# Third experts with a fully split down projection, routing without GpSimd's subtractions, and weights stored as whole 4 KB tiles

## The chip, the cores and the metric

One core of a Trainium2 chip runs the whole program. The metric is the device time of that core in microseconds (us), from the start to the end of one execution. The kernel of before ran three times: 2966.38, 2972.29 and 2977.92 us, median 2972.29.

Engines are named as the profile names them: PE (TensorE, matmuls), PEld (its weight loads), DVE (VectorE), ACT (ScalarE), POOL (GpSimd), SP (SyncE, which issues most DMAs).

## What is computed

The reference runs two different transformer blocks, each of two layers, over 256 tokens of 1024 features, all in float32. The change lies in the first block, mostly in its mixture of experts:

```python
h = rms_norm(x, norm_ffn[l]) * (1.0 + scale_f) + shift_f
grp_idx = top_k(softmax(h @ w_router_grp + b), 1)          # one of 4 groups
top_logit, top_idx = top_k(exp_logits of that group, 2)    # 2 of its 8 experts
for g in range(4):                                         # 32 experts in all
    a, u = h @ w_gate[g], h @ w_up[g]                      # 1024 -> 256
    y += (silu(a) * u * comb[:, g]) @ w_down[g]            # 256 -> 1024
x = x + gate_f * y
```

Ahead of it stands a mixer (`h @ w_in`, attention and gated linear attention, `@ w_out`). The second block has a mixer with its own `w_in_2` and a PEER layer with queries `x @ peer_wq_2` and two tables of 16384 rows.

## The kernel before

**Split products.** PE multiplies float32 in a fast form (F32R) if the operands are rounded. So a weight tile of 128 x 1024 that lands as `raw` is split: ACT copies it rounded to `wh` (L147), DVE or POOL writes `wl = raw - wh` (L150), and PE multiplies with both parts. A weight used without a split ("plain") goes to PE as float32 and costs PE more, but ACT and DVE nothing.

**The stream of weights.** `Stream` knows the order of all weight tiles from a dry run. `load` issues DMAs on SP as soon as a raw buffer is free (10 in the first block, 12 more lent to the experts). `pop` hands out the next tile and, before that, issues the splits of up to `ahead` (4) tiles beyond it, into six pairs of `wh`/`wl`. `prepare(n, engine)` does so at a chosen place and with a chosen engine for the subtraction. Each engine runs its instructions in the order in which they are written; the order of the program is the schedule.

**Planning the experts (`moe_plan`).** Rows are squared and summed on ACT (`square`), X is transposed on PE, four ACT and four DVE instructions (L967, L965) bring it out of PSUM, 32 products with the router weights give the logits (DVE scales them and adds the shift's part at L983). Meanwhile `parts` makes the normalised rows and splits them: two ACT instructions (L957, L958) and one POOL subtraction (L959) per half. Three `prepare` calls split five weight tiles, one subtraction on DVE and four on POOL. `route` (L875 to L898) is a chain of small DVE instructions; its result `m` (L988) is what PE waits for. Then tokens are placed in a sorted order by permutation products (`sorted_half`), and the first expert's gate and up products run between the two halves.

**The experts (`moe_experts`).** The 32 experts of a layer run in one loop, two to a pair `q` that shares 64 rows of sorted tokens. `pick(q + 1)` takes the next pair's rows: an ACT copy (L1120) and a POOL subtraction (L1121) give `hsel`. Six weight tiles belong to an expert: four for gate and up (each 4 x 256 columns in rows of 1 KB in DRAM), two for `w_down`. `expert_down` multiplies the first `w_down` tile split and the second one plain:

```python
parts = w(0)                       # wh, wl: four F32R products of 512 columns
whole = w(1)                       # raw: two float32 products
s.mm(y[n][:SL], h[1], whole[:, n * 512:n * 512 + 512], ...)
```

`hidden` (L1134) makes its other operand: ACT's silu (L1140), DVE's product with the up half (L1141), and the split of the first half of the hidden features alone (L1142, L1143). At e = 1 `weights_of_slots` issues eight DVE instructions (`first`, `gs`, L1178 and L1181) that need a chain of ten small POOL instructions (L1075 to L1084); at e = 2 PE multiplies them, after the gate and up products of half 0 of e = 2. `hsel` of pair 1 is first picked at e = 0, behind those ten POOL instructions on POOL's queue. `most > SL` guards a path (`overflow`) for experts with more than 64 tokens; with these inputs it does not run.

In the trace the planning and the experts take 203 to 532 us in layer 0 and some 691 to 1030 us in layer 1.

## Time and profile before

| | before |
|---|---|
| runs, median (lowest to highest) | 2972.29 us (2966.38 to 2977.92) |
| the profiled execution: its time | 2973.85 us |
| its span, first to last instruction | 2972.1 us |
| PE busy | 2822.3 us, 95% |
| DVE busy | 2235.5 us, 75% |
| ACT busy | 1594.1 us, 54% |
| POOL busy | 490.2 us, 16% |
| mean granted PE clock | 0.968 |
| moved by DMA | 618 MB, 208 GB/s |

Busy means that an instruction of the engine ran. A wait is idle time of an engine that an instruction on another engine ended (the releaser). Only PE's idle time and what stretches its instructions counts directly here; another engine's time counts where PE waits for it. A DMA share is the mean busy share of the core's 16 DMA engines; it can pass 1 where packets overlap.

### The profile page before, as it was taken

Reading aid. Unit: us, or ns where it says so; the run is one execution under the profiler, and the core shown is the slowest. Engines: PE = TensorE matmul, PEld = TensorE weight load, DVE = VectorE, ACT = ScalarE, POOL = GpSimd, SP = SyncE. Lnnn points to the kernel's source line nnn. Section 1 sums busy time; section 2 is a strip of 40 time slices with the busy share of each in tenths; the row PEclk is TensorE's granted clock in tenths of the full one; section 3 lists DMA queues with packets and bytes.
Section 4 is the critical chain, followed back from the end, with each engine's and each line's share of the span. In section 5 each row is a group of like instructions: output and inputs, shape, how many; then the busy total and the mean of one; then the engine's idle time right before and its main releaser. Section 6 shows DMA issues by size and latency. Waiting matters only on the chain. (4 is left out here: it accounts for less than half of the span.)

```text
span 2972.1 us, 48339 instructions
## 1 busy us (share of the span) xinstructions
PE 2822.3 (95%) x18290; PEld 2438.0 (82%) x18291; DVE 2235.5 (75%) x3730; ACT 1594.1 (54%) x2576; POOL 490.2 (16%) x350
## 2 busy tenths in 40 slices
PE   7888999897999989999999999998999999999998
PEld 7766777776777677999999788878799999978886
DVE  7778988767888765898898655566589989865555
ACT  3446777555677546554544444454655554444444
POOL 1222322113322232311000100003331100010000
PEclk9989999998999989999999999998999999999999
DMA  9677998656999442555455555554255554555554
GB/s 355 223 256 259 373 361 301 207 171 228 320 366 360 160 130 72 180 188 175 158 164 169 203 192 191 191 172 138 79 179 188 176 165 162 171 198 191 206 191 149
DMA packets 290588, 618.07 MB, mean 208 GB/s; under 512 B 25168, under 2 KB 159120, under 8 KB 290080
## 3 DMA queue, kind: packets, MB, share of 16 engines
q1 hardware_dynamic: 288816, 608.92, 60.7%
q0 software_dynamic: 1520, 5.87, 0.6%
q8 instruction: 149, 2.44, 0.3%
q14 instruction: 103, 0.84, 0.1%
HBM read 611.30 MB, written 3.15 MB: 207 GB/s over the span
## 5 line engine op out<-in xcount | busy, mean ns | idle before, releaser
L150 DVE TENSOR_TENSOR wl<-raw,wh 128x1024 fp32r<-128x1024 f32 x919 | 1157.5, 1282 | 406.7 <-ACT wh L147 403.0
L147 ACT ACTIVATE wh<-raw 128x1024 fp32r<-128x1024 f32 (+1 forms) x983 | 1006.3, 1050 | 411.9 <-PE pair L245 364.3
L243 PE MATMUL bank<-xth,wh 128*128 128x256 f32 x2048 | 577.0, 282 | 0.0
L245 PE MATMUL bank<-xth,wl 128*128 128x256 f32 x2048 | 571.3, 279 | 0.4 <-DVE wl L150 0.4
L244 PE MATMUL bank<-xtl,wh 128*128 128x256 f32 x2048 | 571.1, 279 | 0.0
L245 PE MATMUL pair<-wh,al 128*128 128x512 f32 x1024 | 401.0, 392 | 10.8 <-DVE al L239 10.8
L243 PE MATMUL pair<-wh,ah 128*128 128x512 f32 x1024 | 403.2, 394 | 1.6 <-ACT ah L238 1.6
L244 PE MATMUL pair<-wl,ah 128*128 128x512 f32 x1024 | 400.9, 392 | 0.0
L245 PEld LDWEIGHTS bank<-xth,wl 128*128 128x128 f32 x2048 | 387.7, 189 | 1.0 <-DVE wl L150 0.8
L243 PEld LDWEIGHTS bank<-xth,wh 128*128 128x128 f32 x2048 | 386.9, 189 | 0.0
L244 PEld LDWEIGHTS bank<-xtl,wh 128*128 128x128 f32 x2048 | 385.5, 188 | 0.0
L248 PE MATMUL bank<-wh,hsel 128*128 128x256 f32 x1024 | 263.7, 296 | 12.8 <-POOL hsel L1121 12.0
L248 PE MATMUL bank<-wl,hsel 128*128 128x256 f32 x1024 | 250.9, 283 | 1.0 <-POOL wl L150 1.0
L248 PEld LDWEIGHTS bank<-wh,hsel 128*128 128x128 f32 x1024 | 194.8, 190 | 67.6 <-issue 25.3
L245 PEld LDWEIGHTS pair<-wh,al 128*128 128x128 f32 x1024 | 192.6, 188 | 57.6 <-DVE al L239 14.1
L243 PEld LDWEIGHTS pair<-wh,ah 128*128 128x128 f32 x1024 | 192.7, 188 | 43.3 <-ACT ah L238 2.3
L244 PEld LDWEIGHTS pair<-wl,ah 128*128 128x128 f32 x1024 | 192.7, 188 | 41.1
L150 POOL TENSOR_TENSOR wl<-raw,wh 128x1024 fp32r<-128x1024 f32 (+2 forms) x67 | 161.0, 2405 | 379.1 <-ACT wh L147 373.0
L248 PEld LDWEIGHTS bank<-wl,hsel 128*128 128x128 f32 x1024 | 195.4, 191 | 2.7 <-POOL wl L150 1.2
L243 PE MATMUL pair<-xth,wh 128*128 128x256 f32 x512 | 150.5, 294 | 0.0
L245 PE MATMUL pair<-xth,wl 128*128 128x256 f32 x512 | 147.4, 288 | 0.7 <-POOL wl L150 0.7
L244 PE MATMUL pair<-xtl,wh 128*128 128x256 f32 x512 | 148.0, 289 | 0.0
(517 smaller groups left out, 4675.5 us busy)
## 6 DMA issues: line engine op xcount, KB each, us to landing
raw<-in_peer_ut SPq DMA_DIRECT2D x256, 512.0 KB, 3.6
raw<-in_peer_v SPq DMA_DIRECT2D x256, 512.0 KB, 3.3
raw<-in_w_gate SPq DMA_DIRECT2D x128, 512.0 KB, 7.5
raw<-in_w_up SPq DMA_DIRECT2D x128, 512.0 KB, 6.9
raw<-in_w_down SPq DMA_DIRECT2D x128, 512.0 KB, 6.2
raw<-in_w_ada SPq DMA_DIRECT2D x96, 512.0 KB, 5.2
raw<-in_w_in SPq DMA_DIRECT2D x80, 512.0 KB, 4.6
raw<-in_w_out SPq DMA_DIRECT2D x32, 512.0 KB, 3.6
```

What stands on the lines that cost most here:

```text
L147: nc.scalar.activation(b, a, AF.Copy)
L150: engine.tensor_tensor(c, a, b.bitcast(F32), op=ALU.subtract)
L243: return [mm(out, lhsT=lh, rhs=rh, start=start, stop=False, skip_group_check=True), mm(out, lhsT=lh, rhs=rl, start=False, stop=False, skip ...
L244: mm(out, lhsT=lh, rhs=rl, start=False, stop=False, skip_group_check=True),
L245: mm(out, lhsT=ll, rhs=rh, start=False, stop=stop, skip_group_check=True)]
L248: s.nc.tensor.matmul(out, lhsT=lhsT, rhs=rhs, start=start, stop=stop, skip_group_check=True)
```

## The change

- Every expert with `e % 3 == 2` (e = 2, 5, ... 29; ten of 32 in each layer) has its second `w_down` tile split as well, and both halves of its hidden features; the other 22 keep the plain product.
- In `moe_plan` the two subtractions of `parts` go to DVE, and both squares and the first half's `parts` go ahead of the transposes' evacuation, the second half's behind it. The `prepare` calls on POOL go away: one tile is split ahead of the route, one after the places of the tokens, two inside `sorted_half(1)`, all on DVE.
- `pick` of pair 1 moves from e = 0 in `moe_experts` to `moe_plan`, behind the first expert's products and ahead of the ten POOL instructions. `hsel1` gets a buffer that outlives the plan.
- `w_gate`, `w_up`, `w_in`, `w_in2` and `peer_wq_2` are laid out by the host so that each tile of 128 x 1024 is one contiguous block with a 4 KB row per partition. Before, a partition's 4 KB came as four pieces of 1 KB (gate, up) or two of 2 KB (the others). The tiles hold the same numbers.

```text
instructions per layer   before                  after
w_down second tile       32 plain                22 plain, 10 split
subtractions of parts    2 on POOL               2 on DVE
early splits             1 on DVE, 4 on POOL     4 on DVE
```

The diff, without the guarded path and the list of input names:

```diff
@@ -353,30 +353,33 @@
         return [(lambda t: t, s.A["w_ada"][l, k * P:(k + 1) * P, j * D:(j + 1) * D])], "plain"
     def w_in(s, name, l, c, n=512):
-        w = s.A[name]
+        w = s.A[name if n == 512 else name + "_rest"]
         def tile_of(i):
+            if n == 512:
+                return [(lambda t: t, w[l, c, i])], 1024
             return [(lambda t: t.rearrange("p (k n) -> p k n", k=2)[:, :, :n],
-                     w[l, i * 256:i * 256 + 256, c * 512:c * 512 + n].rearrange("(k p) n -> p k n", p=P))], \
-                1024 if n == 512 else -n
+                     w[l, i].rearrange("p (k n) -> p k n", k=2))], -n
         return tile_of
     def w_lr(s, l):
-        return [(lambda t: t[:, :128].rearrange("p (k n) -> p k n", k=8),
-                 s.A["w_in"][l, :, 3072:3088].rearrange("(k p) n -> p k n", p=P))], 128
+        return [(lambda t: t[:, :128], s.A["w_lr"][l])], 128
     def w_rows(s, name, l, k):
         return [(lambda t: t, s.A[name][l, k * P:(k + 1) * P, :])], 1024
     def w_expert(s, name, l, e, half):
-        w = s.A[name][l, e % 4, e // 4]
-        return [(lambda t: t.rearrange("p (k n) -> p k n", k=4),
-                 w[half * 512:half * 512 + 512, :].rearrange("(k p) n -> p k n", p=P))], 1024
+        return [(lambda t: t, s.A[name][l, e % 4, e // 4, half])], 1024
     def w_expert_down(s, l, e, k):
-        return [(lambda t: t, s.A["w_down"][l, e % 4, e // 4, k * P:(k + 1) * P, :])], "plain" if k else 1024
+        return [(lambda t: t, s.A["w_down"][l, e % 4, e // 4, k * P:(k + 1) * P, :])], \
+            "plain" if k and s.whole(e) else 1024
+
+    def whole(s, e):
+
+        return e % 3 != 2
     def ada_pe(s, l, j, n):
@@ -956,8 +959,14 @@
             h, lo = (q[:, tt].rearrange("p (k n) -> p k n", k=4) for q in (xh, xl))
             nc.scalar.activation(x, y, AF.Copy, scale=ss[:, tt:tt + 1])
             nc.scalar.activation(h, x, AF.Copy)
-            nc.gpsimd.tensor_tensor(lo, x, h.bitcast(F32), op=ALU.subtract)
+            yield
+            nc.vector.tensor_tensor(lo, x, h.bitcast(F32), op=ALU.subtract)
+            yield
         square(0)
+        square(1)
+        low = parts(0), parts(1)
+        next(low[0])
+        next(low[0])
         banks = s.transposes(s.X)
         for k in range(KT):
             z = banks[k // 2][:, k % 2]
@@ -965,12 +974,9 @@
                 nc.vector.tensor_scalar(ht[:, k], z, g[:, k:k + 1], None, op0=ALU.mult)
             else:
                 nc.scalar.activation(ht[:, k], z, AF.Copy, scale=g[:, k:k + 1])
-        square(1)
+        next(low[1])
+        next(low[1])
         s.st.prepare(1 + ADA_PE, nc.vector)
-        s.st.prepare(2 + ADA_PE, nc.gpsimd)
-        parts(0)
-        parts(1)
-        s.st.prepare(5 + ADA_PE, nc.gpsimd)
         b = s.bank().rearrange("p (t n) -> p t n", t=2)
         for k in range(KT):
             for tt in range(2):
@@ -1048,12 +1054,14 @@
         nc.vector.tensor_copy(oc, pb[:, 2:4])
         each = oc.rearrange("p a (q two) -> p a q two", two=2)
         nc.vector.tensor_copy(offi, each[:, 0, :, 0])
+        s.st.prepare(2, nc.vector)
         next(weights)
         s.table("silu_and_others")
         for _ in sorted_half(0):
             pass
         rest = sorted_half(1)
         next(rest)
+        s.st.prepare(4, nc.vector)
         gu = s.bank()
         s.gate_up(gu, hsel, 0, s.expert_weights(l, 0, 1))
         for _ in rest:
@@ -1062,6 +1070,7 @@
         for j, op in enumerate((ALU.is_lt, ALU.is_ge)):
             nc.vector.tensor_tensor(of_pair[:, j], s.slot[:, 0:1].to_broadcast([P, 16]), each[:, 1, :, 0], op=op)
         s.gate_up(gu, hsel, 1, s.expert_weights(l, 0))
+        following = s.pick(1, hs, offi, mkk)
         next(weights)
         rank, ok, key = mkk([P, 2, 2], "rank"), mkk([P, 2, 2], "ok"), mkk([P, 2, 2], "key")
...
@@ -1131,29 +1140,33 @@
                     s.mm(gu[:, name * 256:name * 256 + 256], hsel[:, k].rearrange("p a q -> p (a q)"), q[:, kk],
                          start=(k == 0 and name == 0 and i == 0), stop=(k == 7 and i == 1))
-    def hidden(s, gs, mk):
+    def hidden(s, whole, gs, mk):
         b = s.bank()[:, :4 * SL].rearrange("p (f q) -> p f q", f=4)
         for f in range(4):
             s.mm(b[:, f], gs[:, f * 128:f * 128 + 128], s.halves, start=(f == 0))
-        a, h = mk([P, 2, SL], "hid", bufs=2), mk([P, 2, SL], "hids", F32R, bufs=2)
+        a, h = mk([P, 2, SL], "hid", bufs=2), mk([P, 2, 2, SL], "hids", F32R, bufs=2)
+        n = 1 if whole else 2
         s.nc.scalar.activation(a, b[:, 0:2], AF.Silu)
         s.nc.vector.tensor_tensor(a, a, b[:, 2:4], op=ALU.mult)
-        s.nc.vector.tensor_copy(h[:, 0], a[:, 0])
-        s.nc.vector.tensor_tensor(h[:, 1], a[:, 0], h[:, 0].bitcast(F32), op=ALU.subtract)
+        s.nc.vector.tensor_copy(h[:, :n, 0], a[:, :n])
+        s.nc.vector.tensor_tensor(h[:, :n, 1], a[:, :n], h[:, :n, 0].bitcast(F32), op=ALU.subtract)
         return h, a[:, 1]
-    def expert_down(s, h, w, y, j):
-
-
-        parts = w(0)
-        for n in range(2):
-            for i, q in enumerate(parts):
-                s.mm(y[n], h[0].rearrange("p a q -> p (a q)"), q[:, n * 512:n * 512 + 512],
-                     start=(j == 0 and i == 0), stop=False)
-        whole = w(1)
-        for n in range(2):
-            s.mm(y[n][:SL], h[1], whole[:, n * 512:n * 512 + 512], start=False, stop=(j == 1))
+    def expert_down(s, h, w, y, j, whole):
+
+
+        for k in range(2):
+            first, last = k == 0 and j == 0, k == 1 and j == 1
+            parts = w(k)
+            for n in range(2):
+                c = slice(n * 512, n * 512 + 512)
+                if k and whole:
+                    s.mm(y[n][:SL], h[1], parts[:, c], start=False, stop=last)
+                    continue
+                for i, q in enumerate(parts):
+                    s.mm(y[n], h[0][:, k].rearrange("p a q -> p (a q)"), q[:, c], start=first and i == 0,
+                         stop=last and i == 1)
     def rows_at(s, idx):
         return idx if s.dry else bass.IndirectOffsetOnAxis(ap=idx, axis=0)
@@ -1209,8 +1222,8 @@
         def down(e):
-            s.expert_down(h, lambda k: s.st.pop(*s.w_expert_down(l, e, k), ahead=None if e < 30 else 63 - 2 * e - k),
-                          yb, e % 2)
+            s.expert_down(h, lambda k: s.st.pop(*s.w_expert_down(l, e, k),
+                                                   ahead=None if e < 30 else 63 - 2 * e - k), yb, e % 2, s.whole(e))
         def weighed(q):
             y, by = [[mk([P, 512], f"y{x}{n}", F32R) for x in "hl"] for n in range(2)], ws[:, q:q + 1]
@@ -1239,8 +1252,10 @@
             if e:
                 gu = s.bank()
                 s.gate_up(gu, hsel, 0, w)
-            if e % 2 == 0 and q < 15:
-                following = s.pick(q + 1, p["hs"], p["offi"], mkk if q % 2 else mk)
+            if e == 0:
+                following = p["following"]
+            elif e % 2 == 0 and q < 15:
+                following = s.pick(q + 1, p["hs"], p["offi"], mkk)
             if e % 2 == 0 and q >= 2:
                 add_all(q - 2)
             if e == 2:
@@ -1266,14 +1281,14 @@
             if e < 31:
                 gn = copied(e, gu)
             if e:
-                h = s.hidden(gs, mk)
+                h = s.hidden(s.whole(e - 1), gs, mk)
             gs = gn
             if e % 2:
                 hsel = following
                 if e < 28:
                     s.adas.tick()
                     s.reduces.tick()
-        last = s.hidden(gs, mk)
+        last = s.hidden(s.whole(31), gs, mk)
         hot = back(15)
         next(hot)
         add_all(14)
...
@@ -2238,9 +2252,23 @@
             nc.scalar.activation(d[:, first:], b[:, first:], AF.Copy, scale=1.0 / GATE)
+def tiles(w, k, n):
+
+
+    lead, (r, c) = w.shape[:-2], w.shape[-2:]
+    w = w.reshape(*lead, r // (k * P), k, P, c // n, n)
+    d = len(lead)
+    w = w.transpose(*range(d), d + 3, d, d + 2, d + 1, d + 4)
+    return np.ascontiguousarray(w).reshape(*lead, c // n, r // (k * P), P, k * n)
+
+
 def lay1(I):
     o = {}
+    o["w_in"] = tiles(I["w_in"][:, :, :3072], 2, 512)
+    o["w_lr"] = tiles(I["w_in"][:, :, 3072:], 8, 16)[:, 0, 0]
+    for name in ("w_gate", "w_up"):
+        o[name] = tiles(I[name], 4, 256)[:, :, :, 0]
     o["c_col"] = np.ascontiguousarray(I["c"].reshape(8, P).T)
     cols = []
     for l in range(2):
@@ -2283,7 +2311,9 @@
     o["cols2"] = np.ascontiguousarray(np.stack(cols))
     o["cmp_pos"] = np.ascontiguousarray(np.stack(pos))
     o["cmp_w1"] = np.ascontiguousarray(np.stack(w1))
-    o["w_in2"] = np.ascontiguousarray(np.stack(w))
+    w = np.stack(w)
+    o["w_in2"], o["w_in2_rest"] = tiles(w[:, :, :2048], 2, 512), tiles(w[:, :, 2048:], 2, 280)[:, 0]
+    o["peer_wq_2"] = tiles(I["peer_wq_2"], 2, 512)
     o["b_row2"] = np.ascontiguousarray(np.stack(rows))
     wo = I["w_out_2"]
     o["w_out2"] = np.ascontiguousarray(wo)
...
```

## Rows read from the trace of the kernel before

**Rows 1.** Busy by stretch (start:end length): PE PEld DVE ACT POOL, clock, DMA, GB/s.

```profile
15.00:20.00 5.00, 4.80 (x23) 4.71 (x24) 3.84 (x3) 0.00 (x0) 0.00 (x0) 1.00 1.02 418
...
232.00:238.00 6.00, 6.00 (x51) 5.76 (x50) 2.21 (x9) 5.08 (x10) 0.00 (x0) 1.00 0.51 169
280.00:300.00 20.00, 19.97 (x117) 14.69 (x116) 19.57 (x23) 13.14 (x18) 6.68 (x3) 1.00 1.07 373
300.00:500.00 200.00, 199.71 (x1187) 151.44 (x1186) 180.16 (x220) 148.45 (x193) 55.51 (x24) 1.00 1.05 364
```

**Rows 2.** PE's waits over the run: total us, times, longest.

```profile
PE bank L248 <- DVE m L988: 21.3, 2, 10.8
PE bank L248 <- POOL hsel L1121: 12.0, 2, 6.3
```

**Rows 3.** Timeline of DVE, routing in layer 0: start us, length us, instruction.

```profile
212.06 0.43 DVE L983 SCALAR_TENSOR_TENSOR lg<-bank,ss,lgc 128x40 f32<-128x40 f32 x2 [0.17 <-PE bank L248]
...
213.01 1.13 DVE L883 CAST gi<-i 128x2 f32<-128x2 uint32 x1
214.18 2.27 DVE L884 TENSOR_TENSOR goh<-iota,gi 128x8 f32<-128x8 f32 x1
216.49 2.33 DVE L887 TENSOR_TENSOR pick<-lg,goh 128x64 f32<-128x64 f32 x1
...
219.76 1.29 DVE L896 CAST ip<-i8b 128x4 f32<-128x4 uint32 x1
221.09 2.25 DVE L897 SCALAR_TENSOR_TENSOR ei<-ip,gi 128x4 f32<-128x4 f32 x1
223.38 2.39 DVE L898 TENSOR_TENSOR oh<-iota,ei 128x128 f32<-128x128 f32 x1
225.81 0.23 DVE L988 TENSOR_TENSOR m<-oh 128x64 bf16<-128x64 f32 x1
225.95 0.28 DVE L989 TENSOR_TENSOR at<-iota,ei 128x128 f32<-128x128 f32 x1
```

**Rows 4.** Timeline of POOL, the same stretch.

```profile
214.07 4.66 POOL L959 TENSOR_TENSOR xl<-hs,xh 128x1024 fp32r<-128x1024 f32 x2
218.69 6.93 POOL L150 TENSOR_TENSOR wl<-raw,wh 128x1024 fp32r<-128x1024 f32 x3
```

**Rows 5.** Timeline of ACT ahead of the logits.

```profile
206.53 1.57 ACT L967 ACTIVATE hs<-bank,affine 128x256 f32<-128x256 f32 x4 [1.12 <-PE bank L518]
207.97 1.07 ACT L951 ACTIVATE xl<-X 128x1024 fp32r<-128x1024 f32 x1
...
211.49 1.13 ACT L957 ACTIVATE hs<-X,ss 128x1024 f32<-128x1024 f32 x1
```

**Rows 6.** Timeline of PE, the products that give the logits.

```profile
207.57 4.45 PE L248 MATMUL bank<-wr,hs 128*128 128x40 f32 x32 [0.48 <-DVE hs L965]
```

**Rows 7.** Timeline of layer 0 around the first pick, POOL, DVE and PE.

```profile
254.05 2.14 POOL L1121 TENSOR_TENSOR hsel<-hs,hsel 128x512 fp32r<-128x512 f32 x2
...
256.59 0.28 DVE L1181 TENSOR_SCALAR gs<-ident,key 128x128 f32<-128x128 f32 x1
...
258.55 0.64 PE L248 MATMUL bank<-oh,first 128*128 128x32 f32 x5
```

**Rows 8.** Timeline of PE, one expert's down projection, and where the next-but-one's ends.

```profile
303.65 0.39 PE L248 MATMUL bank<-wh,hids 128*128 128x512 f32 x1
303.88 0.39 PE L248 MATMUL bank<-wl,hids 128*128 128x512 f32 x1
...
306.52 0.39 PE L248 MATMUL bank<-wh,hsel 128*128 128x256 f32 x1
...
324.06 0.39 PE L248 MATMUL bank<-wh,hsel 128*128 128x256 f32 x1
```

**Rows 9.** DVE's costliest group, 243.4 to 515 us: busy us, mean ns, idle before, releasers.

```profile
L150 DVE TENSOR_TENSOR wl<-raw,wh 128x1024 fp32r<-128x1024 f32 x152 | 191.4, 1323 | 3.0 <-ACT wh L147 2.5 <-DMA raw<-in_w_down 0.4 <-DMA raw<-in_w_gate 0.2
```

**Rows 10.** DVE's waits in the same stretch, 243.4 to 515 us: total us, times, longest.

```profile
DVE hid L1141 <- ACT hid L1140: 19.7, 14, 2.5
```

More of the change, by code (lines that the diff above doesn't have):

```diff
@@ L1096, in moe_plan @@
         return dict(wt=wt, rank=rank, key=key, ow=oh, oc=oc, po=po, pc=pc, offi=offi, of_pair=of_pair, hs=hs, gu=gu,
-                    hsel=hsel, more=more, late=late)
+                    hsel=hsel, following=following, more=more, late=late)
     def expert_weights(s, l, e, ahead=None):
@@ L1314, in overflow @@
                   hid=small[:, 128:128 + 2 * SL].rearrange("p (k q) -> p k q", k=2),
-                  hids=hids[:, :2 * SL].rearrange("p (a q) -> p a q", a=2))
+                  hids=hids[:, :4 * SL].rearrange("p (k a q) -> p k a q", k=2, a=2))
         def mk(shape, name, dt=F32, bufs=1):
@@ L1325, in overflow @@
                 nc.vector.tensor_tensor(mine[:, w, j], small[:, 354:355].to_broadcast([P, 16]), first, op=op)
-        wg = A["w_gate"][l].rearrange("g e d f -> (g e d) f")
-        wu = A["w_up"][l].rearrange("g e d f -> (g e d) f")
+        wg = A["w_gate"][l].rearrange("g e h p n -> (g e h p) n")
+        wu = A["w_up"][l].rearrange("g e h p n -> (g e h p) n")
         wd = A["w_down"][l].rearrange("g e f d -> (g e f) d")
@@ L1349, in of @@
                 def of(half, n):
-                    return part(lambda t: t.rearrange("p (k n) -> p k n", k=4),
-                                (wg, wu)[n][bass.ds(e * 1024 + half * 512, 512), :].rearrange("(k p) n -> p k n", p=P))
+                    return part(lambda t: t, (wg, wu)[n][bass.ds(e * 256 + half * 128, 128), :])
                 nc.vector.tensor_copy(col[:, j:j + 1], mine[:, w, j, bass.ds(q, 1)])
@@ L1356, in more_slots @@
                 nc.vector.tensor_scalar(gs, gu, col[:, j:j + 1], None, op0=ALU.mult)
-                h = s.hidden(gs, mk)
+                h = s.hidden(True, gs, mk)
                 def of_down(k):
@@ L1364, in of_down @@
                     return raw
-                s.expert_down(h, of_down, yb, j)
+                s.expert_down(h, of_down, yb, j, True)
             for n in range(2):
@@ L2323 @@
 RAW1, PARTS1 = 7, 3
-_PLAIN = ["x", "w_ada", "b_ada", "w_in", "w_gk2", "w_out", "w_router_grp", "b_router_grp", "w_router_exp",
-          "b_router_exp", "w_gate", "w_up", "w_down", "lru_wa_2", "lru_wx_2", "cmpk_w2_2",
-          "cmpv_w2_2", "cmpv_b2_2", "ln1_g_2", "ln1_b_2", "peer_wq_2", "peer_v_2", "ln2_g_2", "ln2_b_2"]
+_PLAIN = ["x", "w_ada", "b_ada", "w_gk2", "w_out", "w_router_grp", "b_router_grp", "w_router_exp",
+          "b_router_exp", "w_down", "lru_wa_2", "lru_wx_2", "cmpk_w2_2",
+          "cmpv_w2_2", "cmpv_b2_2", "ln1_g_2", "ln1_b_2", "peer_v_2", "ln2_g_2", "ln2_b_2"]
 def kernel(**inputs):
```

## The prediction, made before the change was run

> **What bounds the kernel now.** I read the busy times by stretch first. In the experts of layer 0, from 300 to 500 us, PE is busy 199.71 of 200 us at full clock [rows 1]: whatever shortens PE's products there shortens the kernel, as long as the others keep up. DVE is next at 180.16 of 200, and from 280 to 300 us it is at 19.57 of 20 [rows 1]. So DVE has a tenth to give in general and nothing in places. Then PE's waits: the two longest kinds lie in the change's path, 21.3 us for `m`, the end of routing, and 12.0 us for the first picked `hsel`, each once per layer [rows 2].
>
> Third, the timeline of DVE under the first of these waits. From the first logit instruction at 212.06 to the end of `m` at 226.04 are 13.98 us, and six instructions on 2 to 128 columns hold 1.13 + 2.27 + 2.33 + 1.29 + 2.25 + 2.39 = 11.66 of them [rows 3]. Right behind, an instruction of the same shape as the last of the six takes 0.28 us [rows 3]. What changes between the two is POOL: its five subtractions run without a gap from 214.07 to 225.62, some 2.3 us each [rows 4], and four of the six stretched instructions last about as long as one of those. So the six wait for POOL's subtractions rather than compute.
>
> **Routing, term A.** Removed: all POOL subtractions in this stretch. The six become 6 x 0.28 = 1.7 us, the chain 13.98 - 11.66 + 1.7 = 4.0 us. Added ahead of the logits: ACT does its second square (1.07 us and three short followers, together an estimate of 1.7) and two copies of half 0 (1.13 each, 2.2) before its evacuations, which had waited 1.12 us for PE anyway [rows 5]; they begin 2.8 us later, at about 209.3. DVE's evacuations stand behind half 0's subtraction (1.3, as any 128 x 1024 one [rows 9]) and end at about 212.3. The logit products, 4.45 us for eight steps [rows 6], follow them and end near 215.0 instead of 212.0. DVE also does half 1's subtraction and one weight tile's before the first logit instruction; ACT delivers half 1 at about 213.1, so DVE is free at 213.1 + 2 x 1.3 = 215.7, 3.6 us later than 212.06. `m` ends at 215.7 + 4.0 = 219.7 instead of 226.04: 6.3 us per layer. Bounds: if nothing of the stretch goes, the 3.6 us are lost; at the other end stands PE's whole wait, 10.7 us a layer [rows 2]. I take 6.3, because the 0.28 us row is of the same shape and only POOL differs.
>
> The other three early subtractions that move from POOL to DVE (3 x 1.3 us) come after the routing, where DVE is busy 2.21 of 6 us while PE runs permutation products [rows 1]. I cost them at nothing; without that cover they cost 3.9 us a layer, in the range below. Behind them on DVE stand the casts of `hsel`, for which PE's first gate product waits. SP's queue is not changed in length, but raw tiles that POOL freed early come free some us later.
>
> **The first pick, term B.** Today its POOL subtraction starts at 254.05, behind ten small POOL instructions [rows 7]; PE waits up to 6.3 us [rows 2]. The change puts it ahead of these ten. Late next is the work of the slots' weights: PE needs DVE's last `gs`, ready at 256.87, and reaches these products today at 258.55 [rows 7]. So PE runs its 16 gate and up products earlier and then waits to about 256.9: 1.7 us of the 6.3 are gained, if the ten POOL instructions are no later. They follow one more weight subtraction on DVE and the pick, so between 0 and 6.3 I take 1.5 per layer, near what the last `gs` allows. ACT's pick copy now stands in front of the first expert's PSUM copy, which is not due yet.
>
> **Ten more split tiles per layer, term C.** A down projection takes 306.52 - 303.65 = 2.87 us on PE, and split products of 512 columns follow each other by 0.23 us [rows 8]. Eight of them are 1.84: 1.0 us less per split expert, 10 us per layer. Price: a subtraction of 1.32 us on DVE [rows 9], the same tile's copy on ACT (74% busy [rows 1]), and hidden features of twice the width (128 columns instead of 64 in a cast and a subtraction; from 0.28 us for 128 columns [rows 3] an estimate of 0.1 us more). That is 1.42 us of DVE per split expert, 14.2 us per layer. DVE's free time between 243 and 515 us is mainly one wait, 19.7 us for ACT's silu, in which it has nothing left to split [rows 10]. So 19.7 - 14.2 = 5.5 us is what DVE can follow of PE's 10. Two experts take 324.06 - 306.52 = 17.5 us [rows 8], three 26.3; in these DVE goes from 23.7 us (its 90% [rows 1]) to 25.1 and PE from 26.3 to 25.3. Bounds 0 and 10; I take 5, because DVE's own sum allows that.
>
> **Layout, term D.** The experts' stretches move 364 to 373 GB/s at a DMA share above 1; the start of the kernel, with 4 KB rows alone, moves 418 at a share of 1.02 [rows 1]. So short rows do cost transfer time. I cost the new layout at nothing: DVE waited for DMA 0.6 us in the whole of layer 0's experts [rows 9], since 22 buffers run ahead; it is PE and DVE that set the pace. If that cover were gone (shorter experts asking for more than the transfers give), the higher ceiling is what holds it off: three experts are 18 tiles, 9.44 MB, and in 25.3 us that is 373 GB/s, the most that the old layout moved. The Trainium skill, DMA: Bandwidth & Descriptors, Specifications, says that transfers from 512 B up already run at line rate. The rows disagree: 373 with 1 KB rows against 418. By that rule the layout gives nothing, the four further tiles of w_ada in the stage would cost an estimate of 1 us of C per layer, and the forecast would be 2949.
>
> **Sum.** 6.3 + 1.5 + 5 = 12.8 us per layer, 25.6 in both (layer 1's two waits are as long [rows 2]). The profiled execution took 2973.85 us, its span 2972.1; 2973.85 - 25.6 = 2948.2. It was 1.56 above the median of the runs, so the forecast against the median is 2946.7, rounded 2947, 0.85% less. About 0.5% is what a measurement of this kernel can tell from no change: the line is 2957.4.
>
> **Rivals.**
> 1. *PE stays the bound.* DVE follows in full, C is 10 per layer: 2 x 17.8 = 35.6 us, 2936.7. For it: DVE at 19.57 of 20 did not hold PE up [rows 1], and six pairs of split buffers smooth its bursts. Against: 25.1 of 25.3 us leaves DVE no reserve for the three or four w_ada accumulations and for its waits in order. 0.17.
> 2. *DVE takes B and C away.* PE waits for `wl` where it waited for nothing; only A is left: 12.6 us, 2959.7. For it: the same 25.1 of 25.3. Against: DVE's 19.7 us of waiting [rows 10] vanish first. 0.16.
> 3. *DVE's new work comes on top.* The place is the hand-over from PE through ACT's silu to DVE once per expert: if DVE's 19.7 us there are a fixed turnaround and not spare time, each split tile lengthens an expert by 1.42 us: +28.4, less A's 12.6: 2988, slower. It decides when less than 14.2 - 6.3 = 7.9 of the 19.7 us can be filled. Against it: these waits fell on 14 experts of some 30 [rows 10], with nothing at the others, which a fixed turnaround does not do. 0.06. The Trainium skill, Perfetto Trace Analysis, Optimizing Scalar/DVE Operations, leans this way: it advises to take work off a saturated VectorE, even to GpSimd, though it adds that the two share a port. Rows 3 and 4 bear out the addition, and in the experts' stretch no run here shows the advice.
> 4. *The change does not do what it says in routing.* If something other than POOL stretches the six, A turns into a loss of 2 x 3.6, and B and C gain 13: 2966.5, the same as before. Against: the 0.28 us row after POOL's end [rows 3, 4]. 0.06.
>
> **How the numbers follow.** The forecast has 0.55 and covers 2938 to 2954; the rivals have 0.17, 0.16, 0.06 and 0.06. The range takes the forecast, most of rival 1 (down to 2930, if A also returns most of its 10.7) and the nearer half of rival 2 (up to 2960): some 0.8. Faster than 2957.4: the forecast, rival 1 and a third of rival 2, 0.78. Within 0.5%: the rest of rival 2 and rival 4, 0.16. Slower: rival 3, 0.06.
>
> **What would show it.** A: the six instructions at 0.2 to 0.3 us, PE's wait for `m` at 4 us or less (from 10.5), the first logit instruction 3 to 4 us later after the last X update. B: no wait for `hsel`, in its place one of some us for `gs` or `first`. C: 20 fewer plain down projections, DVE near 98% in the experts, its wait for silu down to a few us, and PE's first waits for `wl` there. D: more GB/s at a lower DMA share, gate and up tiles landing as fast as `w_down`'s. The prediction is wrong if PE's idle time in the experts passes 10 us a layer, or if the routing chain keeps its microsecond-long small instructions.

## The result, and the profile after

The changed kernel takes 2943.01 us in the median of four runs (2937.31 to 2945.48), beside 2975.11 us for the kernel before in the same job: a ratio of 0.9891, 95% interval [0.9874, 0.9908], or 32 us less. The forecast was 2947 with a range of 2930 to 2960. The execution that was profiled took 2937.31 us, 36.5 less than the profiled one of before.

The page's busy times after:

```profile
span 2935.6 us, 48431 instructions
...
PE 2796.5 (95%) x18290; PEld 2440.9 (83%) x18291; DVE 2248.5 (77%) x3763; ACT 1612.1 (55%) x2596; POOL 455.9 (16%) x337
```

PE's busy time fell by 25.8 us of the span's 36.5: its work became shorter, and a part of its waits went away. Where, the milestones on PE's timeline tell. Each stage below runs from the first PE instruction of one kind to the first of the next, both layers taken from the profiled executions. The last down product is the second `w_down` tile of expert 31:

| stage on PE, us | before, layer 0 / 1 | after, layer 0 / 1 | gain |
|---|---|---|---|
| shift's products to first logit product | 4.12 / 5.41 | 7.26 / 5.78 | -3.1 / -0.4 |
| to the first product with `m` | 18.52 / 18.60 | 10.58 / 8.51 | 7.9 / 10.1 |
| to the first permutation product | 5.83 / 5.89 | 3.72 / 3.74 | 2.1 / 2.2 |
| to the first gate product | 5.08 / 5.08 | 5.94 / 5.95 | -0.9 / -0.9 |
| **A**, sum of these four | 33.55 / 34.98 | 27.50 / 23.98 | 6.0 / 11.0 |
| **B**, to the first split down product | 23.25 / 25.66 | 23.23 / 23.17 | 0.0 / 2.5 |
| **C**, to the start of the last down product | 268.14 / 268.82 | 262.34 / 261.61 | 5.8 / 7.2 |
| to the next stage | 12.45 / 8.56 | 13.32 / 9.61 | -0.9 / -1.0 |

The sum is 11.0 us in layer 0 and 19.7 in layer 1, 30.7 together. The other 5.8 us of the profiled executions lie outside: 6.3 in the second block, 1.0 ahead of layer 0's routing, 1.5 lost in layer 1's mixer. The second block's 6.3 can't be put down to the change: that block took 1940.6 us before, 1934.3 after, and 1950.4 in the experiment below that changes the layout alone (e4), whose median is that of before. So 30.7 is the number to hold against the forecast's 25.6.

**Routing.** The timeline of DVE in layer 0, from the logits to `m` (rows 3 before):

```profile
212.75 1.22 DVE L150 TENSOR_TENSOR wl<-raw,wh 128x1024 fp32r<-128x1024 f32 x1
216.75 0.43 DVE L989 SCALAR_TENSOR_TENSOR lg<-bank,ss,lgc 128x40 f32<-128x40 f32 x2 [2.79 <-PE bank L248]
...
217.70 0.17 DVE L886 CAST gi<-i 128x2 f32<-128x2 uint32 x1
217.90 0.17 DVE L887 TENSOR_TENSOR goh<-iota,gi 128x8 f32<-128x8 f32 x1
218.10 0.22 DVE L890 TENSOR_TENSOR pick<-lg,goh 128x64 f32<-128x64 f32 x1
...
219.27 0.17 DVE L899 CAST ip<-i8b 128x4 f32<-128x4 uint32 x1
219.47 0.16 DVE L900 SCALAR_TENSOR_TENSOR ei<-ip,gi 128x4 f32<-128x4 f32 x1
219.67 0.29 DVE L901 TENSOR_TENSOR oh<-iota,ei 128x128 f32<-128x128 f32 x1
219.99 0.23 DVE L994 TENSOR_TENSOR m<-oh 128x64 bf16<-128x64 f32 x1
```

The six took 11.66 us [rows 3] and now take 1.18. But the chain starts 2.79 us after DVE is free, because PE's logit products are late. The timeline of PE, in layer 0 and in layer 1:

```profile
209.70 7.01 PE L248 MATMUL bank<-wr,hs 128*128 128x40 f32 x32 [3.61 <-DVE hs L974]
...
688.72 4.94 PE L248 MATMUL bank<-wr,hs 128*128 128x40 f32 x32 [0.39 <-DVE hs L974]
```

The same 32 products took 4.45 us before [rows 6]. The window that holds them, in the columns of rows 1:

```profile
209.70:216.50 6.80, 6.80 (x32) 6.80 (x33) 3.48 (x5) 3.73 (x4) 0.00 (x0) 0.51 0.51 183
```

After 3.61 us without work PE is granted 0.51 here, its lower level of 1.2 GHz; in layer 1, with 0.39 us of idling, the products take 4.94. These two rows of the table, the start and the products, make the difference between A's two layers. A pause is not all that goes ahead of a lower clock, though: in layer 1 PE was granted 0.64 from 684 to 688.7 us, where it was busy 4.32 of 4.70 us, and 0.74 in the next 5 us. So the clock falls there without a pause of that length, and why is not shown.

PE's waits in layer 0 from 200 to 260 us (rows 2 before):

```profile
PE bank L248 <- DVE hs L974: 3.6, 1, 3.6
PE bank L248 <- DVE wl L150: 2.3, 2, 1.2
PE bank L248 <- POOL oh L1093: 2.1, 1, 2.1
PE bank L248 <- DVE first L1191: 0.7, 1, 0.7
```

The waits for `m` and `hsel` are gone. In their place stand shorter ones: for the evacuations, for the early splits that DVE now does, and for POOL's last weight instruction. On POOL's timeline the pick of pair 1 now stands ahead of the ten small instructions, of which `oh` is the last:

```profile
239.92 2.48 POOL L1130 TENSOR_TENSOR hsel<-hs,hsel 128x512 fp32r<-128x512 f32 x1 [34.54 <-ACT hsel L1129]
...
248.64 0.40 POOL L1093 TENSOR_TENSOR oh<-oh,wt 128x128 f32<-128x128 f32 x1
```

The pick is done at 242.4 us, some 13 us earlier than before (it is the first of the two in rows 7, and PE began with it at 255.20), and what PE runs into next is `oh`, at 249.1.

**Experts.** The windows of rows 1 again, and below them DVE's longest wait from 243.4 to 515 us (rows 10 before):

```profile
280.00:300.00 20.00, 19.62 (x115) 14.89 (x115) 19.86 (x24) 15.95 (x21) 4.48 (x2) 1.00 0.96 368
300.00:500.00 200.00, 198.20 (x1213) 157.66 (x1212) 193.26 (x234) 158.20 (x205) 53.00 (x24) 1.00 0.96 364
...
DVE hid L1151 <- ACT hid L1150: 5.3, 7, 1.7
```

DVE went from 90% to 97%, its wait for silu from 19.7 to 5.3 us, and PE idles 1.8 us of 200 instead of 0.3. The DMA share fell from 1.05 to 0.96 at the same 364 GB/s.

### The profile page after: what moved, and what is told of

The parts are those of the page before. It is cut to its first block, busy times and chain, and to the rows that moved or that the text cites. A ratio compares the mean times of both kernels' runs of the same rounds, so it can differ in the third digit from the quotient of the medians.

```text
span 2935.6 us, 48431 instructions
## 1 busy us (share of the span) xinstructions
PE 2796.5 (95%) x18290; PEld 2440.9 (83%) x18291; DVE 2248.5 (77%) x3763; ACT 1612.1 (55%) x2596; POOL 455.9 (16%) x337
## 5 line engine op out<-in xcount | busy, mean ns | idle before, releaser
L150 DVE TENSOR_TENSOR wl<-raw,wh 128x1024 fp32r<-128x1024 f32 x948 | 1187.3, 1276 | 406.3 <-ACT wh L147 403.6
L147 ACT ACTIVATE wh<-raw 128x1024 fp32r<-128x1024 f32 (+2 forms) x1003 | 1026.3, 1050 | 421.0 <-PE pair L245 361.7
L150 POOL TENSOR_TENSOR wl<-raw,wh 128x1024 fp32r<-128x1024 f32 (+1 forms) x58 | 139.7, 2409 | 373.1 <-ACT wh L147 368.6
```

The lines of the kernel that those rows point to most:

```text
L147: nc.scalar.activation(b, a, AF.Copy)
L150: engine.tensor_tensor(c, a, b.bitcast(F32), op=ALU.subtract)
```

## The experiments

Eleven kernels ran; each is an edit of the changed kernel but e4, which edits the kernel before. Stage times are those of the table, from one profiled execution each; a single run is told as such. Where expert 31 has its second tile split (e5, e6, e11), the last down product starts 0.7 us into that tile.

**e1, no split added.**

```diff
-        return e % 3 != 2
+        return True
```

> The changed kernel with all 32 second w_down tiles plain again. If DVE took half of the gain (my step), the experts of a layer, from the first down projection to the last, take 5 to 7 us longer than the changed kernel's 262.3 and 261.6, the whole some 12 us more, and DVE's wait for silu is back near 20 us a layer. If PE had stayed the bound, 10 us a layer longer and 20 in all. If the ten splits gained nothing, no difference.

Measured: 2961.04 us, 0.995 [0.9932, 0.9968] of before. Stage C is 269.42 and 268.94 us, 7.1 and 7.3 above the changed kernel's. In the window from 255 to 500 us PE is busy 244.62 of 245 us, where the changed kernel has 242.04:

```profile
255.00:500.00 245.00, 244.62 (x1454) 185.93 (x1453) 223.09 (x275) 181.66 (x237) 67.02 (x30) 1.00 0.96 361
```

So the ten splits gain 7.2 us a layer, C by itself. The whole is 18 us above the changed kernel, 13.7 of them in the two layers. Of the 10 us that ten splits should take off PE [rows 8] 2.8 are missing, and PE's idle time in this window is 2.6 us longer with the splits (245 less 242.04, against 0.38): that is most of it.

What the splits cost DVE is seen over the whole of C. The windows of layer 0, the changed kernel's first and then e1's:

```profile
253.17:515.51 262.34, 259.38 (x1570) 204.92 (x1569) 251.73 (x310) 203.96 (x264) 66.61 (x31) 1.00 0.91 343
...
251.75:521.17 269.42, 269.04 (x1570) 201.68 (x1569) 241.47 (x300) 194.97 (x254) 71.95 (x31) 0.99 0.89 335
```

Ten more subtractions make DVE busy 10.3 us longer, 1.0 us for each split, and leave it 10.6 us of idle time where e1 has 28.0.

**e2, four early splits on POOL**, behind DVE's one and so under the route:

```diff
         s.st.prepare(1 + ADA_PE, nc.vector)
+        s.st.prepare(5 + ADA_PE, nc.gpsimd)
```

> The changed kernel with the four weight tiles behind the first one split early by POOL again, in the routing; the subtractions of the normalised rows stay on DVE. If POOL's subtractions stretch the small DVE instructions, six of them last 1.1 to 2.4 us again, the stretch from the first logit instruction to m goes from 3.5 us to some 10 to 13, and the whole loses 7 to 10 us a layer. If DVE's own order made the difference, the six stay near 0.2 us and nothing is lost.

Measured: 2953.21 us (one run). POOL's timeline, then DVE's:

```profile
213.24 9.53 POOL L150 TENSOR_TENSOR wl<-raw,wh 128x1024 fp32r<-128x1024 f32 x4 [8.72 <-ACT wh L147]
```

```profile
216.82 0.29 DVE L882 MAX8 m<-lg 128x8 f32<-128x8 f32 x2
...
217.43 0.77 DVE L886 CAST gi<-i 128x2 f32<-128x2 uint32 x1
218.23 2.26 DVE L887 TENSOR_TENSOR goh<-iota,gi 128x8 f32<-128x8 f32 x1
220.53 2.32 DVE L890 TENSOR_TENSOR pick<-lg,goh 128x64 f32<-128x64 f32 x1
222.89 0.27 DVE L892 TENSOR_REDUCE sel<-pick 128x16 f32<-128x64 f32 x1
```

With POOL's subtractions the stretch is back, and it ends when they end, at 222.77 us; the three instructions hold 5.35 us instead of 0.56. The other three of the six come after that and are short, so the loss is smaller than was expected: the layers are 4.7 and 7.1 us longer, and the route takes 8.3 us from the first logit instruction to the end of `m`. Stage "to `m`" is 15.41 and 14.94 us, 4.8 and 6.4 longer, and the next one 5.76 and 5.61 (w_ada's products at the lower clock again). The Trainium skill, SBUF — State Buffer, Who interferes with whom, says that a VectorE instruction with two SBUF inputs contends with a GpSimd instruction that reads SBUF, that a copy, a cast or a tensor_scalar can in its two-port modes, where the one that is late is blocked for the whole instruction, and that one with at most one SBUF input outside of these modes does not. The trace agrees: `goh` on 8 columns takes 2.26 us, about one POOL subtraction's length (9.53 us for four), and MAX8 beside POOL takes its usual 0.29 for two. On the other side, from the first gate product to the first down product e2 takes 21.76 and 21.73 us instead of 23.2: the splits that the change moved to DVE cost some 1.45 us a layer there.

**e3, the pick of pair 1 at e = 0 again.**

```diff
-        following = s.pick(1, hs, offi, mkk)
...
-            if e == 0:
-                following = p["following"]
-            elif e % 2 == 0 and q < 15:
+            if e % 2 == 0 and q < 15:
```

> The changed kernel with the first pick back behind the ten small POOL instructions. My step: PE waits some 6 us for hsel again, and the first down projection comes 1 to 2 us later after the first gate product (23.2 us in the changed kernel). Rival, the wait was on the critical path in full: 5 to 6 us later per layer. Rival, it was hidden: no difference.

Measured: 2949.57 us (one run). Of PE's waits over the run:

```profile
PE bank L248 <- POOL hsel L1129: 12.3, 2, 6.2
```

The wait of before returns in full [rows 2], but stage B grows by 1.9 and 3.2 us only (25.15 and 26.40), the second more than the 1 to 2 that were expected: in layer 0 most of the rest of the 6.2 is the time that PE otherwise waits for `oh`, `first` and a second `wl` (2.1, 0.7 and 1.1 us). The whole layer is 1.3 and 2.7 us longer. So the early pick earns some 2.5 us a layer, of which the moved splits take some 1.45 back; 0.0 and 2.5 is what B shows.

**e4, the kernel before with the new layout alone.**

```diff
-        w = s.A[name][l, e % 4, e // 4]
-        return [(lambda t: t.rearrange("p (k n) -> p k n", k=4),
-                 w[half * 512:half * 512 + 512, :].rearrange("(k p) n -> p k n", p=P))], 1024
+        return [(lambda t: t, s.A[name][l, e % 4, e // 4, half])], 1024
...
```

> The kernel before with the new layout of the weights alone. My step: no difference that can be measured, under 0.2%, with the stages' lengths within 1 us of before and gate and up tiles landing as fast as those of w_down. Rival, the transfers held the second block or the mixers up: the span shorter by 6 us or more, most of it outside of the experts, as the changed kernel's second block was 6.3 us shorter in the profiled execution.

Measured: 2973.27 us, 1.0002 [0.998, 1.0024] of before. Every stage of the planning and the experts is within 0.5 us of before.

**e5 and e6, all 32 and 16 second tiles split.**

```diff
-        return e % 3 != 2
+        return False                 # e5
+        return e % 2 == 0            # e6
```

> The changed kernel with every second w_down tile split, 32 of 32. If DVE is the bound of the experts by now, 22 more tiles cost it 22 x 1.4 = 31 us a layer, of which its last 5 us of waiting for silu take some: the stretch from the first to the last down projection grows from 262 to 283 to 290 us a layer, PE waits 30 us or more for wl, and the whole loses 40 to 55 us. If PE still sets the pace, the stretch falls by up to 22 us a layer.

> The changed kernel with every second expert's second w_down tile split, 16 of 32 per layer instead of 10. DVE gets 6 x 1.4 = 8.5 us more a layer and has some 5 us of waiting left: if it is the bound from here on, the stretch of the experts stays between 261 and 266 us (262.3 in the changed kernel), with its wait for silu near zero. If PE still set the pace, 256 us.

Measured (one run each): 2959.69 us for e5, 2944.3 for e6. The window from 255 to 500 us of e5, and PE's waits in it:

```profile
255.00:500.00 245.00, 221.11 (x1418) 192.70 (x1417) 242.87 (x296) 205.26 (x260) 42.87 (x30) 0.99 0.95 357
...
PE bank L248 <- DVE hids L1153: 10.9, 13, 1.4
PE bank L248 <- DVE wl L150: 4.6, 3, 1.6
PE bank L248 <- ACT gs L1244: 4.2, 9, 1.3
```

Here the bound has moved: DVE is busy 242.87 of 245 us and never waits for silu, and PE waits for it, for `hids` more than for `wl`. The layers are 8.6 and 11.6 us longer than with ten splits, C (273.25 and 273.93 us) 10.2 and 11.6 to the same point of the last tile, about half of what was expected of it. With 16, C is 263.70 and 262.48, or 0.7 and 0.2 more than with ten to the same point: the six splits more gain nothing there. The best number lies somewhere between ten and 16, as far as single runs show, and it is flat there.

**e7, another order of the planning**: the transposes' evacuations before `parts(0)`, DVE's subtraction of half 1 and one tile's after the logits and the places, ACT's gates and table ahead.

```diff
         low = parts(0), parts(1)
-        next(low[0])
-        next(low[0])
         banks = s.transposes(s.X)
...
-        next(low[1])
-        next(low[1])
-        s.st.prepare(1 + ADA_PE, nc.vector)
+        next(low[0])
+        next(low[0])
+        next(low[1])
...
         places(0)
+        next(low[1])
+        s.st.prepare(1, nc.vector)
         places(1)
```

> The changed kernel with another order in the routing: ACT and DVE bring the transposes out of PSUM first and make the normalised rows afterwards; the second half's subtraction and the first weight tile's move behind the places of the first half, and the exponentials and the table load of ACT ahead of the places. The same instructions otherwise. If the 3.6 us of PE's idle time ahead of the logits and the slow products behind it are the cost of the chosen order, layer 0 gains 5 to 8 us from the shift's products to the first gate product (27.5 us in the changed kernel) and layer 1 1 to 2 us (24.0), the whole 6 to 10 us against the changed kernel. If the chain is held by something else, nothing changes.

Measured: 2935.04 us, 0.9871 [0.9855, 0.9888] of before. The layers take 319.75 and 316.56 us, 6.6 and 1.8 less than the changed kernel's 326.39 and 318.37. PE's timeline in layer 0, and the window of these products:

```profile
206.61 3.77 PE L248 MATMUL bank<-wr,hs 128*128 128x40 f32 x32 [0.77 <-DVE hs L972]
...
206.60:211.00 4.40, 4.39 (x34) 4.06 (x35) 2.90 (x9) 4.34 (x6) 0.00 (x0) 1.00 1.03 409
```

PE waits 0.77 us for the evacuations and not 3.61, keeps its full clock, and does the products in 3.77 us and not 7.01. That is 3.24 + 2.84 = 6.1 of the 6.6 us. A is 22.32 and 23.17 us, 5.2 and 0.8 less; 1.7 of layer 0's gain is lost again at w_ada's eight products, which take 5.38 us behind a wait of 1.78 us for `m`. Layer 1 falls short of the 1 to 2 us that were expected.

**e8, the two subtractions of `parts` on POOL.**

```diff
-            nc.vector.tensor_tensor(lo, x, h.bitcast(F32), op=ALU.subtract)
+            nc.gpsimd.tensor_tensor(lo, x, h.bitcast(F32), op=ALU.subtract)
```

> The changed kernel with the two subtractions of the normalised rows on POOL again, the weight tiles still on DVE. These two end before the logits are there. If only an overlap in time with the chain of small DVE instructions costs, nothing is lost in layer 0 and under 1.5 us in layer 1. If any POOL subtraction in the routing costs, m comes 3 us or more later in both.

Measured: 2948.37 us (one run); the layers are 1.0 us shorter and 1.9 longer. POOL's and DVE's timelines in layer 0:

```profile
206.08 2.36 POOL L963 TENSOR_TENSOR xl<-hs,xh 128x1024 fp32r<-128x1024 f32 x1 [3.25 <-ACT xh L961]
209.66 2.35 POOL L963 TENSOR_TENSOR xl<-hs,xh 128x1024 fp32r<-128x1024 f32 x1 [1.22 <-ACT xh L961]
```

```profile
206.45 1.66 DVE L974 TENSOR_SCALAR hs<-bank,affine 128x256 f32<-128x256 f32 x4 [3.84 <-ACT hs L976]
210.56 2.54 DVE L150 TENSOR_TENSOR wl<-raw,wh 128x1024 fp32r<-128x1024 f32 x1 [2.45 <-ACT wh L147]
```

The evacuations from PSUM run beside POOL at their usual 1.66 us; a tile's subtraction doubles from 1.22 to 2.54, yet both subtractions of POOL are over, at 212.01, before the route's small instructions begin. What mattered was not that POOL worked but that it worked under the route. Layer 1 lost more than the 1.5 us that were allowed for. There the route's small instructions are as short as ever, but DVE's stretched subtraction ahead of them ends at 689.12 us, 11.9 us after the shift's products, where the changed kernel has its first logit instruction 10.8 us after them: that is 1.1 of the 1.9 us.

**e9, the changed kernel with the layout of before.** The edit is e4's, read backwards.

> The changed kernel with the weights laid out as before (gate and up tiles in rows of 1 KB, the others in rows of 2 KB); all else as changed. With the layout alone the time stood at 1.0002 [0.998, 1.0024] of before, but there the experts asked for less: in the changed kernel's window of 245 us PE is busy 242.04 us and moves 364 GB/s at a DMA share of 0.96, where the old rows needed 1.05 for the same rate. My theory (22 raw buffers run ahead, so the transfers are hidden in both): 2940 to 2949 us, 0.988 to 0.992, the stretch from the first to the last down projection at 262 to 264 us, DVE's wait for DMA in the window under 2 us. The rival (the faster experts need the higher ceiling, so the layout is what lets term C be earned): the stretch at 265 to 270 us, 6 to 16 us for both layers, 2950 to 2960 us, and DVE and ACT waiting some us for raw tiles.

Measured: 2945.69 us, 0.9896 [0.9875, 0.9916] of before. C takes 263.04 and 262.17 us, 0.7 and 0.6 more. The window of rows 1, and the page's DMA issues (median us from issue to landing last):

```profile
300.00:500.00 200.00, 198.21 (x1213) 157.70 (x1212) 193.22 (x234) 157.31 (x203) 51.84 (x24) 1.00 1.04 364
...
raw<-in_w_gate SPq DMA_DIRECT2D x128, 512.0 KB, 7.8
raw<-in_w_down SPq DMA_DIRECT2D x128, 512.0 KB, 6.7
```

and the changed kernel's issues:

```profile
raw<-in_w_gate SPq DMA_DIRECT2D x128, 512.0 KB, 6.7
raw<-in_w_down SPq DMA_DIRECT2D x128, 512.0 KB, 6.0
```

The layout makes tiles land 0.7 to 1.1 us sooner and the queues 8% less busy for the same bytes, and PE is busy 198.21 us in one and 198.20 in the other. The medians lie 2.7 us apart, well inside both intervals: a gain from the layout isn't seen, though one below a us in C couldn't be told from nothing here.

**e10, e7's order with 12 splits.** The expectation counts 13; the condition below splits experts 1, 3, 6, 8 and so on to 28, which are 12.

```diff
-        return e % 3 != 2
+        return e % 5 not in (1, 3) or e == 31
```

> The changed kernel with the order of e7 (transposes brought out first, ACT's table and gates ahead) and 13 of the 32 second down tiles split in place of 10. One more split takes some 0.65 us off PE (6.8 us for ten between no split and ten) and puts some 1.4 us on DVE, which waits 5.4 us for silu in the window of 245 us of the run with ten and 1.4 us in that with 16. Theory (PE sets the pace until DVE's waiting is used up, and that is about so at 13): stretch from first to last down projection 260 to 262 us where e7 has 262.5 and 262.3, the whole 2929 to 2935 us, 0.985 to 0.987. Rival (DVE's bursts cost PE as much as a split gives from ten on, as 16 splits gave 263.7 and 262.5): 262 to 264 us, 2934 to 2940, no difference from e7.

Measured: 2937.37 us, 0.9875 [0.9854, 0.9895] of before; C takes 262.98 and 261.09 us, where e7 has 262.53 and 262.26. The time doesn't differ from e7's, as the rival had it; of C's two layers one lies in the rival's range and one in the theory's. The expectation's 6.8 us for ten splits is 7.2 by the table.

**e11, e6 with every sixth split's subtraction on POOL in the experts.**

```diff
-        s.st.on_pool = 0
+        s.st.on_pool = 6
```

> The changed kernel with 16 second down tiles split (as e6, 2944.3 us) and, in the experts, the subtraction of every sixth split on POOL in place of DVE: some 26 in the window of 245 us, 26 x 1.25 = 33 us off DVE, which was busy there 241.4 us. One theory (the Trainium skill, Perfetto Trace Analysis, Optimizing Scalar/DVE Operations: work taken off a saturated VectorE, even to GpSimd, helps): DVE's busy time 205 to 215 us, PE's waits for hids and gs gone (3.0 and 1.7 us in e6), stretch from first to last down projection 257 to 260 us where e6 has 263.7 and 262.5, the whole 2932 to 2940 us. Rival, mine (as in the routing of before, each POOL subtraction of some 2.3 us stretches what DVE does meanwhile, and its tile is ready a us later): DVE's busy time falls by less than half of the 33 us, small instructions among hid, hids and the 1024-column subtractions get longer than 0.3 and 1.25 us, PE's waits stay, stretch 262 to 268 us, the whole 2942 to 2956 us.

Measured: 2996.7 us (one run), 52 us above e6; C takes 286.76 and 289.95 us, worse than even the rival's 262 to 268. From 255 to 500 us, the window, POOL's and DVE's costliest groups, and PE's longest wait:

```profile
255.00:500.00 245.00, 227.55 (x1362) 182.19 (x1362) 233.26 (x243) 184.54 (x236) 101.09 (x52) 0.98 0.90 338
...
L150 POOL TENSOR_TENSOR wl<-raw,wh 128x1024 fp32r<-128x1024 f32 x24 | 66.5, 2772 | 112.0 <-ACT wh L147 112.0
...
L150 DVE TENSOR_TENSOR wl<-raw,wh 128x1024 fp32r<-128x1024 f32 x119 | 176.2, 1538 | 4.9 <-ACT wh L147 3.5 <-DMA raw<-in_w_down 1.0
...
PE bank L248 <- DVE hids L1153: 6.9, 9, 1.8
```

POOL took 24 subtractions off DVE, and DVE's remaining ones grew from a mean of 1245 ns (e6, the same group) to 1538. DVE stays busy 233 us for 119 tiles, where e6 had 157 done in 241. The Trainium skill, Perfetto Trace Analysis, Optimizing Scalar/DVE Operations, says that it may make sense to move work off a saturated VectorE, even to GpSimd, and warns that the two may not gain from it, as they share a port. Here the move costs 52 us (one run of each), and the longer subtractions on DVE agree with the warning.

## Why the prediction was right

**A, routing: 6.3 a layer forecast, 6.0 and 11.0 measured.** The mechanism holds: the six instructions went to 1.18 us (forecast 1.7), and POOL under the route brings the stretch back (e2). Two terms were missing or mis-sized and nearly cancel in layer 0, so that 6.0 comes so near 6.3 is luck. "The logit products, 4.45 us for eight steps, follow them" was the step that failed there: they took 7.01 us, at the lower clock after PE had idled, and so PE and not DVE set the start of the route (DVE waited 2.79 us for it, and the first logit instruction came 14.3 us after the shift's products instead of 8.6: 5.7 us later, where 3.6 were forecast). The other missing term works the other way. The wait for `m` had left PE at its lower level: eight products of w_ada behind it took 5.78 us before, and 3.68 now. The windows that hold them, and the products, before:

```profile
226.00:232.00 6.00, 5.77 (x20) 2.71 (x20) 4.47 (x18) 0.87 (x3) 0.54 (x3) 0.59 0.80 272
...
226.71 5.78 PE L248 MATMUL pair<-raw,cc 128*128 128x512 f32 x8
```

and after:

```profile
220.20:224.30 4.10, 3.87 (x21) 1.97 (x20) 3.57 (x14) 0.00 (x0) 0.00 (x0) 1.00 0.57 148
...
220.88 3.68 PE L248 MATMUL pair<-raw,cc 128*128 128x512 f32 x8
```

These 2.1 us a layer were not counted; 0.9 of them are given back at once, as PE now reaches the permutation ahead of ACT (a wait of 0.60 us for `hs`). In layer 1 DVE set the start, as forecast, but A came to 11.0, just above the upper bound of 10.7. The first logit instruction on DVE there, after and before:

```profile
693.70 0.43 DVE L989 SCALAR_TENSOR_TENSOR lg<-bank,ss,lgc 128x40 f32<-128x40 f32 x2
...
703.19 0.42 DVE L983 SCALAR_TENSOR_TENSOR lg<-bank,ss,lgc 128x40 f32<-128x40 f32 x2
```

The shift's products start at 682.94 and 693.47 us, so the added work ahead of the logits delays the route by 10.76 - 9.72 = 1.0 us in layer 1, and not by 3.6: that term was worked out for layer 0 and taken for both. It makes 2.6 us of the 4.7 by which A passes the forecast there. Nor is 11.0 a firm number: in six of the kernels above (e1, e3, e5, e6, e9, e11), whose planning ahead of the gate products is the changed kernel's, A takes 27.5 to 27.6 us in layer 0 but 23.7 to 26.2 in layer 1, which is 8.8 to 11.3 less than before. The slowest of them, e9, is granted 0.50 from 681 to 698 us there.

**The early splits on DVE, costed at nothing: 1.45 us a layer (e2).** The cover I named, DVE's free time under the permutation products, was there, but the first expert's gate and up products wait for `wl` twice, 1.2 and 1.1 us.

**B, the first pick: 1.5 a layer forecast, 0.0 and 2.5 measured.** By itself the early pick earns 1.9 and 3.2 (e3), somewhat over the 1.7 of the working; the moved splits take their 1.45 out of the same stage. That something else is late next was named, but not what: DVE's `gs` or `first` was expected, and it is POOL's `oh`, 2.1 us, the last of the ten small instructions, and only then `first`, 0.7 us.

**C, ten splits: 5 a layer forecast, 5.8 and 7.2 measured, 7.1 and 7.3 against e1.** That DVE would follow PE a part of the way was right. The step "5.5 us is what DVE can follow of PE's 10" was too strict, by both of its terms. PE's busy time in C fell by 9.7 us (e1), near the 10 of the working. But a split makes DVE busy 1.0 us longer and not 1.42, and DVE had 28.0 us of idle time to fill in C (e1), of which the 19.7 of its longest wait are a part. That this wait fell by 14.4 us, close to the 14.2 that the working put into it, does not bear out that price. PE lost 2.6 us to waits from 255 to 500 us, and DVE stood at 97% there. Rival 1, all of it, would have been 10. Rival 2 and rival 3 were ways in which DVE takes the gain; e5 shows that DVE does take it at 32 splits (8.6 to 11.6 us lost a layer), and e6 that more splits than ten gain nothing more by 16.

**D, the layout: nothing forecast, nothing measured** (e4: 1.0002; e9 0.9896 beside the changed kernel's 0.9891). Rows of 1 KB do cost transfer time, a share of 1.04 against 0.96 at 364 GB/s; it is hidden. The Trainium skill's figure of the 512 B (DMA: Bandwidth & Descriptors, Specifications) would have forecast the same for the layout, by another reason, and the shares speak against that reason. The 1 us of C a layer that the forecast put beside that figure rests on no row; e9's C is 0.7 and 0.6 us longer, which one execution can't tell from nothing.

**Sum.** 30.7 us in the two layers against 25.6: 4.7 more in layer 1's A and 3.0 in the two C, 0.3 less in layer 0's A, 0.5 less in the two B, and 1.9 lost behind the last down products, a stage that the forecast did not name; why it is longer is open. PE's idle time in the experts is 3 us of 245, far from the 10 that would have made the forecast wrong. Rival 4 is out: something other than POOL would have left the six as they were.

The experiments also point to a kernel that beats the changed one in its medians: e7's, 0.9871 against 0.9891, though the two intervals overlap; the 8.4 us by which its two profiled layers are shorter are read from one execution of each.

## What to carry to other kernels

Small VectorE instructions that last microseconds are a sign to look for what GpSimd does in the same microseconds; move the GpSimd work out of that stretch, not necessarily off GpSimd. When a step is moved ahead of products, ask whether PE idles meanwhile: the wait can be paid twice, once as time and once more as slower products behind it. And before DVE is given what PE sheds, add up all of its idle time in the stretch, not one wait alone: the 28.0 us here paid for ten splits, and 16 gained nothing more.

## What the runs showed of the hardware

- A pause of 3.61 us on PE was followed by 6.8 us at a granted 0.51; one of 0.77 us (e7), by full clock. The same 32 products took 7.01 and 3.77 us. In layer 1 the clock was lower (0.74) behind a pause of 0.39 us, so the length of the pause alone does not tell it.
- Beside POOL's subtractions of 2.3 us DVE's small instructions on two SBUF operands were stretched to 2.3 or 2.4 us, whatever their width (8 columns as well as 128, before and in e2), and casts to 0.8 to 1.4 us; MAX8 (e2) and an instruction that reads PSUM (e8) were not.
- In the experts POOL's subtractions took 2772 ns each, and DVE's grew from 1245 to 1538 ns, so that the two engines did fewer tiles in 245 us, 24 and 119, than DVE alone, 157 (e6, e11).
